# mLSTM heads: score order, the denominator's bank, table loads, and 1/sqrt by Ln and Exp

## The chip, the cores and the metric

One core of a Trainium2 chip runs the program; the other cores are idle. The metric is the device time of one execution in microseconds. The kernel before took 900.06 us, the median of three runs (899.17 to 901.06).

## What is computed

Two layers over 512 tokens of 1024 channels in fp32. The even layer makes one projection that feeds two groups of heads: A, four mLSTM heads of width 256, and B, eight stick-breaking attention heads of width 128. The odd layer is a pooling mixer. The change lies in group A:

```
q, k = silu(causal_dwconv(...)); ig, lf = gates
Sc  = (q k^T / 16) * W              # W = exp of gate sums, causal
num = Sc v ; den = sum over s of Sc
h   = num / max(|den|, exp(-m))
u   = sigmoid(oa) * h
ya  = u * rsqrt(mean(u*u) + eps) * hn_g * silu(za)
```

The kernel computes a head over all 512 tokens at once, without the chunks of the reference. With floor = exp(-m) and d = max(|den|, floor) it never divides by d: u is formed as num * sigmoid(oa), and the norm takes dd = mean(u*u) + eps*d*d, so that u / sqrt(dd) is the wanted quotient.

## The kernel before, in words

The token axis lies on the free dimension (512 columns, one PSUM bank), channels or keys on the 128 partitions. Every fp32 product is made of three fp32r matmuls over a high and a low half of each operand (mm3: L112 high x high, L113 high x low, L114 low x high). `split` makes the halves: ScalarE copies the high half (L88), VectorE subtracts it (L89).

PSUM's eight banks are shared out by tag: pj (2, projections), sc (2, scores), ac (2, accumulators), xa and xb (1 each). In the A stage xa serves `den` and the product "psb" of the two Strassen projections, xb serves "pse" and the mean `mn`; "psa" uses pj.

The loop at L722 runs over the four heads. For each: the projections of q and k (ps_qa), their causal convolution of four taps on VectorE (L428) and a Silu, then a Cast and a subtraction for the halves (L432, L433); the gate rows are loaded into `bc`; `values` projects v (psv_va, four blocks of 128 tokens, each split at L453); `mlstm`; `mlstm_den`; the output gate oa and the gate path za by `strassen2` (seven half-size products each, named psa, psb, pse); and `mlstm_out`. Values of head 0 are projected ahead of its q and k.

`mlstm` goes over four key blocks si. A block's scores s are six matmuls into a bank of tag sc, the tokens before the block left out (512, 384, 256 and 256 columns). ScalarE makes w = exp(bc + cT) (L476), VectorE multiplies it by the scores (L478), which is the last reader of the score bank, `split` makes ph and pl, and six matmuls add to the two num banks. GpSimd adds the w of all blocks (L492); that sum is split into dh and dl, and two matmuls by a matrix of ones make den (L495, L496). `mlstm_den` reads den with an Abs on ScalarE (L501).

`mlstm_out` takes the Sigmoid of o, forms u and its square mean (mn, L519 and L520), adds to dd (L521), takes the Sqrt on ScalarE and the reciprocal on VectorE (L523), the Silu of z, and stores the result in DRAM.

The order of work: a scheduler walks the program with a simulated clock, and each engine gets a fixed list from it; a tile with a tag waits until a buffer of that tag is free. `tc.add_manual_dep(later, earlier, NOSYNC)` adds an edge to that planning; on one engine it fixes the order of two instructions. Every activation that needs a table goes through `act`, which puts an ACT_TABLE_LOAD in front when the table set changes (L69) and links all of them in program order. Copy, Abs and Square go past `act` and need no load. In the kernel before, `last["ins"]` can name an instruction behind which the next table load must stand; it is set in one place only, at the end of the even layer (L800).

Of the kernel before, what the change touches and what calls it, by code (L numbers as in the profile page):

```python
# [9 lines left out]
AF = mybir.ActivationFunctionType  # L10
# [3 lines left out]
NOSYNC = mybir.DependencyInfo(mybir.DependencyClass.NoSync, mybir.DependencyReason.DATA)  # L14

P = 128
# [10 lines left out]
HA, HB = 4, 8  # L27
# [11 lines left out]
def body(nc, tc, x, pre_g, post_g, w_in, conv, b_i, b_f, hn_g, w_out, w_in_c, pool_w,  # L39
# [6 lines left out]
    with base as base, psum as psum, dram as dram:  # L46
# [5 lines left out]
        def sc(name): return bank("sc", 2, name)  # L52
        def ac(name): return bank("ac", 2, name)
        def xa(name): return bank("xa", 1, name)
# [1 line left out]

        table, last = {"ins": None, "set": None}, {}

        def link(i):
            if table["ins"] is not None:
# [3 lines left out]
        def act(dst, src, func, **kw):  # L66
            if table["set"] != TABLE[func]:
                table["set"] = TABLE[func]
                i = A.preload_act_table_set(TABLE[func])  # L69
                link(i)  # L70
                if "ins" in last:
                    tc.add_manual_dep(i.ins, last.pop("ins").ins.name, NOSYNC, reason="table order")
            i = A.activation(dst, src, func, **kw)
            link(i)
            return i
# [11 lines left out]
        def split(src, hi, lo, name=None):  # L87
            high[name] = A.activation(hi, src, AF.Copy)  # L88
            low[name] = V.tensor_tensor(lo, src, hi.bitcast(F32), op=ALU.subtract)  # L89
# [19 lines left out]

        def mm3(dst, lhs, rhs, first, last, **kw):  # L110
            (ah, al), (bh, bl) = lhs, rhs
            T.matmul(dst, lhsT=ah, rhs=bh, start=first, stop=False, **kw)  # L112
            T.matmul(dst, lhsT=ah, rhs=bl, start=False, stop=False, **kw)  # L113
            T.matmul(dst, lhsT=al, rhs=bh, start=False, stop=last, **kw)  # L114

        hTh = base.tile([P, 8, S], F32R, name="hTh")
        hTl = base.tile([P, 8, S], F32R, name="hTl")
# [192 lines left out]
        def phi(name): return at.tile([P, S], F32R, tag="phi", bufs=4, name=name)  # L310
        def plo(name): return at.tile([P, S], F32R, tag="plo", bufs=4, name=name)
# [124 lines left out]
        def values(col, name, with_gates=False):  # L436
            vh, vl = vtile(name)
            n = 264 if with_gates else 256

            def parts(t):  # L440
                yield nc.sync, t[:, :, :256], w_in[0, :, col:col + 256]
                if with_gates:
                    yield A, t[:, :, 256:], w_in[0, :, GI:GI + 8]
            w8 = load(parts, 8, n, name)
            w = [halves(w8[:, 4 * j:4 * j + 4], f"{name}{j}") for j in range(2)]
            for tt in range(NB):
                ps = pj(f"psv_{name}{tt}")
                for k in range(8):
                    wh, wl = w[k // 4]
                    ts = slice(tt * P, tt * P + P)  # L450
                    mm3(ps[:, :n], (hTh[:, k, ts], hTl[:, k, ts]),
                        (wh[:, k % 4], wl[:, k % 4]), k == 0, k == 7)
                split(ps[:, :256], vh[:, tt], vl[:, tt])  # L453
                if with_gates:
                    V.tensor_copy(gates[:, tt], ps[:, 256:n])
            return vh, vl
# [7 lines left out]

        def mlstm(h, q, k, v, bc):
            num = [ac(f"num{h}{j}") for j in range(2)]
            den = xa(f"den{h}")
            for si in range(NB):
                t0 = P * si
                n0 = min(t0, 256)  # L470
                s = sc(f"s{h}{si}")
                for j in range(2):
                    mm3(s[:, n0:], tuple(a[:, t0:t0 + P] for a in k[j]),
                        tuple(a[:, n0:] for a in q[j]), j == 0, j == 1)
                w = tmp(f"w{h}{si}")
                act(w[:, t0:], bc[:, ROW[si]:ROW[si] + S - t0], AF.Exp,  # L476
                    bias=cT[:, si, h:h + 1])
                V.scalar_tensor_tensor(w[:, t0:], s[:, t0:], 1.0 / 16.0, w[:, t0:],  # L478
                                       op0=ALU.mult, op1=ALU.mult)
                ph, pl = phi(f"ph{h}{si}"), plo(f"pl{h}{si}")  # L480
                if n0 < t0:
                    G.memset(ph[:, n0:t0].bitcast(F32), 0.0)
                    G.memset(pl[:, n0:t0].bitcast(F32), 0.0)
                split(w[:, t0:], ph[:, t0:], pl[:, t0:])
                first, last = si == 0, si == NB - 1
                for j in range(2):
                    mm3(num[j][:, n0:], tuple(a[:, si, j * P:j * P + P] for a in v),
                        (ph[:, n0:], pl[:, n0:]), first, last)
                if si == 0:
                    total = w  # L490
                else:
                    G.tensor_tensor(total[:, t0:], total[:, t0:], w[:, t0:], op=ALU.add)  # L492
            ph, pl = phi(f"dh{h}"), plo(f"dl{h}")
            split(total, ph, pl)
            T.matmul(den, lhsT=ones, rhs=ph, start=True, stop=False)  # L495
            T.matmul(den, lhsT=ones, rhs=pl, start=False, stop=True)  # L496
            return num, den
# [8 lines left out]
        def mlstm_out(h, num, dd, o, z):  # L506
            mn = xb(f"mn{h}")
            for j in range(2):
                act(o[j], o[j], AF.Sigmoid)
            us, squares = [], []  # L510
            for j in range(2):
                us.append(tmp(f"u{h}{j}"))
                squares.append(tmp(f"u2{h}{j}"))
                V.tensor_tensor(us[j], num[j], o[j], op=ALU.mult)
                A.activation(squares[j], us[j], AF.Square)
            V.tensor_tensor(squares[0], squares[0], squares[1], op=ALU.add)
            ph, pl = phi(f"uh{h}"), plo(f"ul{h}")
            split(squares[0], ph, pl)
            T.matmul(mn, lhsT=mean256, rhs=ph, start=True, stop=False)  # L519
            T.matmul(mn, lhsT=mean256, rhs=pl, start=False, stop=True)  # L520
            V.tensor_tensor(dd, mn, dd, op=ALU.add)  # L521
            act(dd, dd, AF.Sqrt)
            V.reciprocal(dd, dd)  # L523
            for j in range(2):
                c = 2 * h + j
                act(z[j], z[j], AF.Silu)
                V.scalar_tensor_tensor(us[j], us[j], hg(c), dd, op0=ALU.mult, op1=ALU.mult)
                V.tensor_tensor(z[j], us[j], z[j], op=ALU.mult)
                G.dma_start(ydr[:, c], z[j])
# [192 lines left out]
        for h in range(HA):  # L722
            if h == 0:
                v = values(VA, "va0")
            q, k = ([conv_silu(ps, co + 2 * h + j, f"{off}_{2 * h + j}") for j, ps in
                     enumerate(project2(w_in[0, :, off + 256 * h:off + 256 * h + 256],
                                        f"qa{off}_{h}"))] for off, co in ((QA, 0), (KA, 8)))
            bc = at.tile([P, EN + S], F32, tag="bc", bufs=1, name=f"bc{h}")
            nc.sync.dma_start(bc, rdr[h].partition_broadcast(P))
            for s in range(NB):  # L730
                t = bc[:, ROW[s]:ROW[s] + P]
                G.affine_select(t, t, pattern=[[1, P]], base=0, channel_multiplier=-1,
                                compare_op=ALU.is_ge, fill=-1e30)
            if h:
                v = values(VA + 256 * h, f"va{h}")
            num, den = mlstm(h, q, k, v, bc)
            dd = mlstm_den(h, den, bc)
            o, z = ([ozt(f"r_{n}{h}_{j}") for j in range(2)] for n in ("oa", "za"))
            if h == HA - 1:
                ready = y_split(y_back(tmp)(0, EVEN[0]), (qkt("yh_early"), qkt("yl_early")))  # L740
            for t, off, n in ((o, OA, "oa"), (z, ZA, "za")):
                strassen2(at, hs, w_in[0, :, off + 256 * h:off + 256 * h + 256], f"{n}{h}", t)
            mlstm_out(h, num, dd, o, z)
# [25 lines left out]
        with tc.tile_pool(name="odd", bufs=1) as od:  # L769
# [21 lines left out]
            def finish_even(ps, tt):  # L791
                xt = big(f"xe{tt}")
                nc.sync.dma_start(xt, xr[:, tt])
                t = big(f"xse{tt}")
                post(ps, t, gpo, xt, xn[:, tt], f"e{tt}")
                n0 = tt % 2 * P
                i = [copy() for copy in prenorm(xn[:, tt], t, tt, [gpr[:, :512], gpr[:, 512:]], f"p1{tt}", 1,
                            lambda i: y32[:, tt // 2 * 8 + 4 * i:tt // 2 * 8 + 4 * i + 4, n0:n0 + P])]
                if tt == NB - 1:
                    last["ins"] = i[-1]  # L800

            for a in range(2):
                finish_even(ps0[a], a)
# [112 lines left out]
```

## Time and profile before

| | |
|---|---|
| median of three runs | 900.06 us (899.17 to 901.06) |
| profiled execution | 899.45 us, span 897.5 us, granted TensorE clock 0.999 |
| TensorE matmul busy | 884.0 us (98%) |
| VectorE busy | 640.1 us (71%) |
| ScalarE busy | 521.1 us (58%), 28 table loads of 1.28 us |
| GpSimd busy | 99.0 us (11%) |

The span is from the first instruction to the last; the profiled execution's own time has 1.95 us around it. Matmuls are pipelined: a matmul's row shows when it starts and a modelled duration, and the next one starts before that is over. How far apart two starts are is therefore the time that a matmul takes in a full stream. The heads of group A take from about 250 to 500 us.

### The profile page before, as it was taken

To read this page: it belongs to the slowest core of one execution; us is meant where nothing else is said; L and a number is where in the kernel's file an instruction comes from. 1 tells how busy PE (TensorE), PEld (TensorE's weight loads), DVE (VectorE), ACT (ScalarE), POOL (GpSimd) and SP (SyncE) were. 2 spreads that over 40 slices of the span, in tenths; PEclk is the share of its full clock that TensorE was granted. 3 is DMA by queue.
4 is the path that set the end of the run, shared out by engine and by line. 5 is a ranking of instruction groups with operands and counts; after the bars stand their busy time and mean duration, and the time that the engine had idled before them with its cause. 6 is when DMAs were issued, how large, how long until landed. Compare 5 with 4: busy or idle time off the path is not lost.

```text
span 897.5 us, 13390 instructions
## 1 busy us (share of the span) xinstructions
PE 884.0 (98%) x5195; PEld 777.4 (87%) x5195; DVE 640.1 (71%) x969; ACT 521.1 (58%) x888; POOL 99.0 (11%) x209
## 2 busy tenths in 40 slices
PE   8999999999999999999999999999999999999997
PEld 6888889889988889999899888898999999988885
DVE  6655556567877697796796856779789897956542
ACT  7646676766766656746746835676455454655331
POOL 1001011101112101001001000005012120300000
PEclk9999999999999999999999999999999999999999
DMA  8231322222313431522422677641334242347331
GB/s 283 95 95 51 92 93 73 80 85 71 95 48 112 136 118 47 183 71 89 141 71 75 243 230 298 214 139 48 94 95 142 86 134 64 111 148 244 107 118 47
DMA packets 73202, 106.89 MB, mean 119 GB/s; under 512 B 3409, under 2 KB 59817, under 8 KB 73138
## 3 DMA queue, kind: packets, MB, share of 16 engines
q1 hardware_dynamic: 70240, 101.27, 34.1%
q0 software_dynamic: 1280, 4.20, 1.2%
q8 instruction: 41, 0.67, 0.3%
q10 hardware_dynamic: 1618, 0.56, 0.3%
q14 instruction: 23, 0.19, 0.1%
HBM read 99.70 MB, written 6.32 MB: 118 GB/s over the span
## 4 chain that ended last, share of the span: by engine, by line
PE 97%; DVE 1%; ACT 1%; issue 0%; POOL 0%; DVEq 0%; ACTq 0%; POOLq 0%
PE op L653 10%; PE oq L653 10%; PE ps_qa L112 3%; PE ps_qa L113 3%; PE ps_qa L114 3%; PE psv_va L112 2%; PE psv_va L114 2%; PE psv_va L113 2%; PE ps_zb L112 2%; PE mx L114 2%; PE mx L112 2%; PE mx L113 2%; PE ps_zb L114 2%; PE ps_kb L112 2%; PE ps_qb L114 2%; PE ps_kb L114 2%
## 5 line engine op out<-in xcount | busy, mean ns | idle before, releaser
L112 PE MATMUL ps_qa<-hTh,wh_qa 128*128 128x512 f32 x128 | 50.3, 393 | 0.0
L113 PE MATMUL ps_qa<-hTl,wh_qa 128*128 128x512 f32 x128 | 50.3, 393 | 0.0
L114 PE MATMUL ps_qa<-hTh,wl_qa 128*128 128x512 f32 x128 | 50.2, 393 | 0.0
L89 DVE TENSOR_TENSOR wl_wo_e<-w_wo_e,wh_wo_e 128x1024 fp32r<-128x1024 f32 x28 | 33.7, 1222 | 14.9 <-ACT wh_wo_e L88 14.7
L839 POOL TENSOR_TENSOR s<-s,invc 128x1 f32<-128x1 f32 (+3 forms) x16 | 22.2, 1385 | 188.6 <-DVE s L836 82.0
L88 ACT ACTIVATE wh_wo_e<-w_wo_e 128x1024 fp32r<-128x1024 f32 x28 | 28.9, 1055 | 22.4 <-DMA w_wo_e<-in_w_out_ab 14.3
L69 ACT ACT_TABLE_LOAD x28 | 35.9, 1283 | 1.8 <-PEq L901 1.4
L114 PE MATMUL psv_va<-wh_va,hTl 128*128 128x256 f32 x128 | 36.1, 282 | 0.0
L113 PE MATMUL psv_va<-wl_va,hTh 128*128 128x256 f32 x128 | 36.1, 282 | 0.0
L112 PE MATMUL psv_va<-wh_va,hTh 128*128 128x256 f32 x128 | 36.1, 282 | 0.0
L653 PE MATMUL op<-wl_wo_e,yh_e 128*128 128x512 f32 x112 | 36.1, 396 | 0.0
L653 PE MATMUL op<-wh_wo_e,yl_e 128*128 128x512 f32 x112 | 35.7, 395 | 0.0
L428 DVE SCALAR_TENSOR_TENSOR cv<-u,vecs,cv 128x511 f32<-128x511 f32 (+2 forms) x48 | 35.3, 738 | 0.1
L653 PE MATMUL op<-wh_wo_e,yh_e 128*128 128x512 f32 x112 | 34.8, 398 | 0.0
L89 DVE TENSOR_TENSOR wl_wo_o<-w_wo_o,wh_wo_o 128x1024 fp32r<-128x1024 f32 x20 | 24.2, 1223 | 11.0 <-ACT wh_wo_o L88 11.0
L653 PE MATMUL oq<-wh_wo_o,yl_o 128*128 128x512 f32 x96 | 30.6, 395 | 0.0
L653 PE MATMUL oq<-wl_wo_o,yh_o 128*128 128x512 f32 x96 | 30.5, 395 | 0.0
L653 PE MATMUL oq<-wh_wo_o,yh_o 128*128 128x512 f32 x96 | 29.6, 395 | 0.0
L88 ACT ACTIVATE wh_wo_o<-w_wo_o 128x1024 fp32r<-128x1024 f32 x20 | 20.8, 1053 | 15.2 <-PE oq L653 6.9
L112 PEld LDWEIGHTS ps_qa<-hTh,wh_qa 128*128 128x128 f32 x128 | 24.1, 188 | 5.4 <-ACT r_za L306 0.4
L114 PEld LDWEIGHTS ps_qa<-hTh,wl_qa 128*128 128x128 f32 x128 | 24.1, 188 | 5.2
L113 PEld LDWEIGHTS ps_qa<-hTl,wh_qa 128*128 128x128 f32 x128 | 24.1, 188 | 5.1
(559 smaller groups left out, 3238.0 us busy)
## 6 DMA issues: line engine op xcount, KB each, us to landing
w_wo_e<-in_w_out_ab SPq DMA_DIRECT2D x14, 1024.0 KB, 4.9
w_wo_o<-in_w_out_c SPq DMA_DIRECT2D x12, 1024.0 KB, 5.0
w_qa<-in_w_in_ab SPq DMA_DIRECT2D x8, 1024.0 KB, 4.9
w_p<-in_w_in_c SPq DMA_DIRECT2D x8, 1024.0 KB, 5.1
w_z<-in_w_in_c SPq DMA_DIRECT2D x8, 1024.0 KB, 5.0
w_qb<-in_w_in_ab SPq DMA_DIRECT2D x4, 1024.0 KB, 5.2
w_kb<-in_w_in_ab SPq DMA_DIRECT2D x4, 1024.0 KB
w_zb<-in_w_in_ab SPq DMA_DIRECT2D x4, 1024.0 KB
```

Source lines behind the costliest of these rows:

```text
L69: i = A.preload_act_table_set(TABLE[func])
L88: high[name] = A.activation(hi, src, AF.Copy)
L89: low[name] = V.tensor_tensor(lo, src, hi.bitcast(F32), op=ALU.subtract)
L112: T.matmul(dst, lhsT=ah, rhs=bh, start=first, stop=False, **kw)
L113: T.matmul(dst, lhsT=ah, rhs=bl, start=False, stop=False, **kw)
L114: T.matmul(dst, lhsT=al, rhs=bh, start=False, stop=last, **kw)
L428: V.scalar_tensor_tensor(acc[:, j:], u[:, :S - j], cw(3 - j, c), acc[:, j:], op0=ALU.mult, op1=ALU.add)
L653: T.matmul(ps[a][n], lhsT=l[:, ta], rhs=r[:, 0, n * 512:n * 512 + 512], start=(first and l is yh and r is wh), stop=(last and l is yl))
L839: G.tensor_tensor(sm[:, :e], sm[:, :e], invc[:, :e], op=ALU.mult)
```

## The change

- `mm3` returns its three matmuls. In `mlstm` an edge puts the first score matmul of block 1 behind the last one of block 0.
- `den` is taken from tag sc, after the four blocks, instead of from xa.
- `last` is renamed `hold` and set in two more places: in `mlstm` after every block's split (`high[None]` is the ScalarE copy of the last unnamed `split`), so that the head's next table load, that of the Sigmoid, stands behind the split of block 3; and, in heads 1 and 2, after `values`, so that the load for the head's Exps stands behind the split of the last block of values.
- `mlstm_out` makes 1/sqrt(dd) as exp(-ln(dd)/2) with two activations of one table set, instead of a Sqrt and a reciprocal.

```
         def mm3(dst, lhs, rhs, first, last, **kw):
             (ah, al), (bh, bl) = lhs, rhs
-            T.matmul(dst, lhsT=ah, rhs=bh, start=first, stop=False, **kw)
-            T.matmul(dst, lhsT=ah, rhs=bl, start=False, stop=False, **kw)
-            T.matmul(dst, lhsT=al, rhs=bh, start=False, stop=last, **kw)
+            return [T.matmul(dst, lhsT=ah, rhs=bh, start=first, stop=False, **kw),
+                    T.matmul(dst, lhsT=ah, rhs=bl, start=False, stop=False, **kw),
+                    T.matmul(dst, lhsT=al, rhs=bh, start=False, stop=last, **kw)]
...
         def mlstm(h, q, k, v, bc):
             num = [ac(f"num{h}{j}") for j in range(2)]
-            den = xa(f"den{h}")
             for si in range(NB):
...
-                for j in range(2):
-                    mm3(s[:, n0:], tuple(a[:, t0:t0 + P] for a in k[j]),
-                        tuple(a[:, n0:] for a in q[j]), j == 0, j == 1)
+                mms = [m for j in range(2)
+                       for m in mm3(s[:, n0:], tuple(a[:, t0:t0 + P] for a in k[j]),
+                                    tuple(a[:, n0:] for a in q[j]), j == 0, j == 1)]
+                if si == 1:
+                    tc.add_manual_dep(mms[0].ins, done.ins.name, NOSYNC, reason="order of scores")
+                done = mms[-1]
...
                 split(w[:, t0:], ph[:, t0:], pl[:, t0:])
+                hold["ins"] = high[None]
...
+            den = sc(f"den{h}")
             ph, pl = phi(f"dh{h}"), plo(f"dl{h}")
...
             V.tensor_tensor(dd, mn, dd, op=ALU.add)
-            act(dd, dd, AF.Sqrt)
-            V.reciprocal(dd, dd)
+            act(dd, dd, AF.Ln)
+            act(dd, dd, AF.Exp, scale=-0.5)
...
             if h:
                 v = values(VA + 256 * h, f"va{h}")
+                if h < HA - 1:
+                    hold["ins"] = high[None]
```

## Rows read from the trace of the kernel before

**Rows 1.** The page's busy times: busy us, share of the span, instructions.

```profile
PE 884.0 (98%) x5195; PEld 777.4 (87%) x5195; DVE 640.1 (71%) x969; ACT 521.1 (58%) x888; POOL 99.0 (11%) x209
```

**Rows 2.** TensorE's waits, 270 to 500 us: who for whom, us, times, longest.

```profile
PE s L112 <- DVE w L478: 2.6, 4, 0.7
PE psb_oa L112 <- ACT dd L501: 0.7, 1, 0.7
PE psb_za L112 <- DVE r_oa L291: 0.5, 1, 0.5
```

**Rows 3.** Timeline of TensorE, head 1: start us, duration, instruction [idle before, releaser].

```profile
342.66 0.40 PE L112 MATMUL s<-h,h 128*128 128x512 f32 x1
...
344.89 0.57 PE L114 MATMUL s<-h,l 128*128 128x512 f32 x2
345.30 0.39 PE L112 MATMUL s<-h,h 128*128 128x512 f32 x1
...
346.12 0.57 PE L114 MATMUL s<-h,l 128*128 128x512 f32 x2
347.38 0.39 PE L112 MATMUL s<-h,h 128*128 128x256 f32 x1 [0.68 <-DVE w L478]
347.60 0.28 PE L113 MATMUL s<-l,h 128*128 128x256 f32 x1
...
348.90 0.28 PE L112 MATMUL psa_oa<-n2h,wh_oa_b 128*128 128x256 f32 x1
...
350.32 0.63 PE L112 MATMUL num<-ph,vh_va 128*128 128x512 f32 x2
...
354.08 0.28 PE L114 MATMUL num<-ph,vl_va 128*128 128x256 f32 x1
```

**Rows 4.** Timeline of TensorE, head 0.

```profile
287.15 0.28 PE L114 MATMUL psa_za<-hTh,wl_za_a 128*128 128x256 f32 x1
287.99 0.39 PE L112 MATMUL s<-h,h 128*128 128x256 f32 x1 [0.57 <-DVE w L478]
...
296.47 0.40 PE L496 MATMUL den<-dl,ones 128*128 128x512 f32 x1
297.56 0.39 PE L112 MATMUL psb_oa<-hTh,wh_oa_a 128*128 128x256 f32 x1 [0.69 <-ACT dd L501]
...
298.97 0.28 PE L114 MATMUL psb_oa<-hTh,wl_oa_a 128*128 128x256 f32 x1
299.76 0.39 PE L112 MATMUL psb_za<-hTh,wh_za_a 128*128 128x256 f32 x1 [0.52 <-DVE r_oa L291]
```

**Rows 5.** Timeline of VectorE, head 1.

```profile
346.63 1.16 DVE L478 SCALAR_TENSOR_TENSOR w<-s,w 128x512 f32<-128x512 f32 x2 [1.82 <-PE s L114]
...
354.74 0.69 DVE L89 TENSOR_TENSOR dl<-w,dh 128x512 fp32r<-128x512 f32 x1 [1.02 <-ACT dh L88]
```

**Rows 6.** Timeline of ScalarE, head 1.

```profile
342.39 0.62 ACT L73 ACTIVATE cv<-cv 128x512 f32<-128x512 f32 x1
343.02 1.28 ACT L69 ACT_TABLE_LOAD   x1
344.32 1.93 ACT L73 ACTIVATE w<-bc,cT 128x512 f32<-128x512 f32 x4
346.26 1.28 ACT L69 ACT_TABLE_LOAD   x1
347.55 0.39 ACT L88 ACTIVATE vh_va<-psv_va 128x256 fp32r<-128x256 f32 x1
```

**Rows 7.** Groups of instructions by line: busy us, mean ns, idle before.

```profile
L523 DVE RECIPROCAL dd<-dd 128x512 f32<-128x512 f32 x4 | 13.4, 3346 | 0.0
```

**Rows 8.** Timeline of ScalarE, end of head 0 and start of head 1.

```profile
314.85 0.64 ACT L73 ACTIVATE dd<-dd 128x512 f32<-128x512 f32 x1
...
325.58 0.62 ACT L73 ACTIVATE cv<-cv 128x512 f32<-128x512 f32 x1
```

**Rows 9.** Busy times by stretch: length, PE, PEld, DVE, ACT, POOL (instructions), TensorE clock, DMA.

```profile
320.00:340.00 20.00, 20.00 (x129) 18.16 (x128) 20.00 (x33) 7.61 (x14) 1.46 (x4) 1.00 0.24 79
```

More of the change, by code (lines that the diff above doesn't have):

```diff
@@ L55, in xb @@
         def xb(name): return bank("xb", 1, name)
-        table, last = {"ins": None, "set": None}, {}
+        table, hold = {"ins": None, "set": None}, {}
         def link(i):
@@ L70, in act @@
                 link(i)
-                if "ins" in last:
-                    tc.add_manual_dep(i.ins, last.pop("ins").ins.name, NOSYNC, reason="table order")
+                if "ins" in hold:
+                    tc.add_manual_dep(i.ins, hold.pop("ins").ins.name, NOSYNC, reason="table order")
             i = A.activation(dst, src, func, **kw)
@@ L799, in finish_even @@
                 if tt == NB - 1:
-                    last["ins"] = i[-1]
+                    hold["ins"] = i[-1]
             for a in range(2):
```

## The prediction

> **What bounds the kernel now.** I read the page's busy shares first: TensorE is busy for 884.0 of the 897.5 us [rows 1]. Only what takes a wait or a matmul off TensorE's own list can shorten the run, and all the edits lie in the mLSTM stage. So the next view was TensorE's waits between 270 and 500 us. The reader is to see that there are six in all: four at the third score block of a head (score bank, waiting for VectorE's L478), one at psb_oa (waiting for ScalarE's Abs of the denominator) and one at psb_za (waiting for VectorE's L291) [rows 2]. They sum to 3.8 us between modelled ends and starts. The timeline says what they really take, because in a full stream matmuls start closer together than they last. A pair of 512 and 384 columns takes 0.41 us (344.89 to 345.30; two such pairs from there to 346.12), which by columns is 0.23 and 0.175; twelve of 256 columns take 1.42 (348.90 to 350.32), 0.12 each [rows 3].
>
> Head 1 [rows 3]: the pair of score matmuls at 346.12 is followed only at 347.38, 1.26 us later, so 0.85 is lost. The restarted matmul then takes 0.22 us to the next instead of 0.12, so 0.10 more. That is 0.95 us in head 1. Of the 2.6 us that the list gives to the four waits, 0.68 is head 1 and 0.57 head 0; the 1.35 left is 0.68 for each of heads 2 and 3, so I take 0.95 there too. In head 0 [rows 4] it is 287.99 - 287.15 - 0.12 = 0.72, and 0.10 for the restart: 0.82. After the denominator, 297.56 - 296.47 - 0.23 = 0.86 and 0.10: 0.96. Before psb_za, 299.76 - 298.97 - 0.12 = 0.67 and 0.10: 0.77. All six: 0.82 + 3 x 0.95 + 0.96 + 0.77 = 5.40 us. More than this the change can't give back.
>
> **Scores in order (edges from the last matmul of block 0 to the first of block 1).** No instruction is added. Today blocks 0 and 1 alternate, so that block 0 ends only one matmul ahead of block 1, and VectorE's L478 on block 0, which frees the bank for block 2, begins when TensorE has nothing left. In the new order all six matmuls of block 1 stand behind block 0's last. From the start of block 0's last matmul: VectorE begins 0.51 us later (346.12 to 346.63), needs 0.75 until TensorE can go on (346.63 to 347.38), 1.26 in all. TensorE meanwhile does that matmul and six of 384 columns: 0.23 + 6 x 0.175 = 1.28. The wait just vanishes, with nothing to spare, so I leave a restart of 0.10 in each head: gain 0.82 + 2.85 - 0.40 = 3.27 us. Block 3 comes behind block 2's six matmuls (0.7 us), while L478 on block 1, 384 columns wide, ends about 0.46 us after the first one (the pair takes 1.16 [rows 5]): no wait there.
>
> **Denominator in a score bank.** The two den matmuls write another bank; psb_oa no longer waits for ScalarE to read den: 0.96 us in head 0. Den needs the sum of all four w, so every L478, the last reader of the score banks, is over before it can start, and the next user of its bank is the next head's block 0: no wait is added. In heads 1 to 3 other products stand between den and psb_oa today and nothing waits [rows 2], so nothing is gained there. The 0.77 before psb_za stays in the sum: it is the one bank xa handed from one product to the next, and the edit does not touch that. It is the low end of the range.
>
> **Table loads.** Their number stays four a head. The Sigmoid load stands today between the Exps and the splits (346.26 [rows 6]); behind the last split it makes these 1.28 us earlier and itself later, and whatever follows in ScalarE's list has the same work ahead of it as before. No TensorE wait names those splits [rows 2], so there is nothing to gain; the other end is 4 x 1.28 = 5.1 us lost, if TensorE came to wait for what stands behind the load in each head. I take 0, by the unchanged amount of work. In heads 1 and 2 the Exp load moves behind the last values split. That split runs after the Silu ending at 343.01: split to 343.41, load to 344.69, first Exp of 512 columns (0.64) to 345.35, against 344.32 + 0.64 = 344.96 now. Queued behind it on ScalarE are the four Exps; VectorE's L478 waits for them. With the scores where they are now, block 0's last matmul starts at 344.89 + 3 x 0.23 = 345.58 and L478 can begin at 346.09, so 0.7 us of cover is left: cost 0. If that cover is gone the price is in the first rival below.
>
> The row shows no more than the load itself: Silu ends 343.01, load starts 343.02, first Exp 344.32, 0.02 us after the load's end [rows 6]. The Trainium skill (ScalarE: Activation LUTs, What ACT_TABLE_LOAD costs) gives a switch 1283 ns for the load and about 1380 ns of drain, 2.66 us; the load agrees with the trace, the drain is not there. By that rule the first Exp would end at 346.73, L478 start at 346.78 and block 2 at 347.53 instead of 346.86: 0.67 and 0.10 lost in each of two heads, and the time 897.3.
>
> **Ln and Exp for Sqrt and reciprocal.** VectorE loses 4 x 3.35 = 13.4 us [rows 7]; ScalarE gets four more 512-column activations of 0.64 (the Sqrt's row [rows 8]), 2.6 us. The chain from dd to its use becomes 0.64 + 3.35 - 2 x 0.64 = 2.7 us shorter a head, but no TensorE wait names what follows. The Silu load and the two Silus come 0.64 us later. Today they end at about 314.85 + 0.64 + 1.28 + 2 x 0.62 = 318.0, and the next Silu in the fixed order starts at 325.58 [rows 8], so 7.5 us hide it. VectorE has no idle time in the 20 us after the reciprocal [rows 9] and TensorE waits for none of its work there, so a lighter VectorE gives it nothing at once. It may bring the last key's halves forward by up to 2.7 us, and what that can cost is rival A. Late next, once the waits are gone, is L478 on block 0 again, which has nothing to spare.
>
> **Sum.** 3.27 + 0.96 = 4.23 us. The profiled execution took 899.45 (span 897.5 and 1.95 around it): 895.2. It was 0.6 under the median of the runs, 900.06, so as a median: 895.8. All six waits gone would be 894.7.
>
> **Rivals.**
> A. The held Exp load takes the place of the bank wait. Lighter VectorE makes the keys ready up to 2.7 us sooner, so heads 1 and 2 can issue blocks 0 and 1 without the 12 product matmuls (1.42 us) that now stand between 342.66 and 344.89. Then block 0 ends near 344.2 and block 1's slots end at 342.66 + 6 x 0.23 + 6 x 0.175 = 345.09, but L478 waits for the Exp until 345.40 and block 2 for L478 until 346.15: 1.06 + 0.10 = 1.16 lost instead of 0.95. Against the forecast 2 x (1.16 - 0.10) = 2.1 us: 897.9. For it: the cover is 0.7 us and VectorE is full just before. Against it: with xa free, psb_oa (12 matmuls) is one more product that can stand there. 0.18; the table drain, with the row against it, 0.02.
> B. No change: the list is planned anew from a simulated clock, and new waits of about 1 us turn up in as many places as were removed. For it: today's four are such misses of a plan. Against it: elsewhere in 225 us this planner left only the waits listed. About 900.0; 0.15.
> C. Slower: fill is spent early. Between the last score and the first num stand 12 product matmuls (348.90 to 350.32), and between the last num (354.08) and the end of the denominator's low half (354.74 + 0.69 = 355.43) others fill 1.2 us [rows 3, 5]. The free xa bank lets products go ahead sooner; if these two gaps are left bare in heads 1 to 3, each head loses 1.4 + 1.2 + 0.2 of restarts = 2.8, together 8.4: 895.8 + 8.4 = 904.2. It decides from 1.4 us a head, half of that. Against it: the two Strassen projections are fourteen products a head, and psb_oa comes behind den today [rows 4]. 0.09.
>
> **How the numbers follow.** Forecast 0.56, A and the drain 0.20, B 0.15, C 0.09. About 0.2%, 1.8 us, is what a measurement here can tell from no change; faster by more (under 898.3) is the forecast and A: 0.76. Same 0.15, slower 0.09. The range goes from all six waits gone with a run 0.8 below the median, 893.9, up past A to within B, 899.9; about 0.17 lies above it.
>
> **What would show it.** TensorE's list of waits for the stage: L112 on L478 gone or at most 0.1 a head, psb_oa on ScalarE gone; psb_za may remain. All of block 0 ahead of block 1 in each head. 28 table loads as now, the Sigmoid load behind the four ph splits. No reciprocal of 512 columns, VectorE some 13 us less busy, ScalarE 2.6 more. Rival A shows as L112 waiting for L478, and L478 for an Exp; C as num or den waiting for a split. The prediction is wrong if TensorE's waits in the stage sum to more than 2 us, or if the saving comes from outside it.

## The result, and the profile after

The changed kernel takes 895.0 us (median of four runs, 894.49 to 895.55) against 899.8 us for the kernel before on the same chip: a ratio of 0.9937, 95% interval 0.9925 to 0.9949. The forecast was 895.8. The profiled execution has a span of 892.4 us, 5.1 less than before.

The page's busy times (busy us, share of the span, instructions): TensorE does the same work and VectorE 13.3 us less. ScalarE's busy time is unchanged, where 2.6 us more were forecast: its activations of dd do take 2.5 us more (9.9 against 7.4), but busy time counts rows that overlap only once, and what took up the difference was not traced.

```profile
PE 883.2 (99%) x5195; PEld 777.8 (87%) x5195; DVE 626.8 (70%) x965; ACT 521.1 (58%) x892; POOL 99.6 (11%) x209
```

TensorE's waits of the changed kernel from 270 us to the end (who for whom, us in total, times, longest). All six of [rows 2] are gone, and what is left lies in the odd layer, where it was before:

```profile
PE ps_p L112 <- ACT hTh L88: 0.2, 1, 0.2
PE ps_p L113 <- DVE hTl L89: 0.2, 1, 0.2
PE ps_p L112 <- ACT p L830: 0.2, 1, 0.2
```

Head 1 in TensorE's timeline, against [rows 3]. Block 0 (341.06 on), block 1 (342.45 on), then 12 matmuls of the product psa_oa, then block 2 (344.94), with no idle time:

```profile
341.06 0.40 PE L112 MATMUL s<-h,h 128*128 128x512 f32 x1
...
342.21 0.39 PE L114 MATMUL s<-h,l 128*128 128x512 f32 x1
342.45 0.34 PE L112 MATMUL s<-h,h 128*128 128x384 f32 x1
...
343.51 0.28 PE L112 MATMUL psa_oa<-hTh,wh_oa_a 128*128 128x256 f32 x1
...
344.94 0.28 PE L112 MATMUL s<-h,h 128*128 128x256 f32 x1
```

ScalarE (against [rows 6]) and VectorE (against [rows 5]) in that head. The last values split (341.26) now stands ahead of the Exp load, the Sigmoid load (348.07) behind the four ph splits, and the last key's low half is done at 337.96, 3.1 us before the first score:

```profile
341.26 0.38 ACT L88 ACTIVATE vh_va<-psv_va 128x256 fp32r<-128x256 f32 x1 [0.36 <-PE psv_va L114]
341.66 1.28 ACT L69 ACT_TABLE_LOAD   x1
342.95 1.92 ACT L73 ACTIVATE w<-bc,cT 128x512 f32<-128x512 f32 x4
...
347.45 0.61 ACT L88 ACTIVATE ph<-w 128x256 fp32r<-128x256 f32 x2
348.07 1.28 ACT L69 ACT_TABLE_LOAD   x1
```

```profile
337.27 0.69 DVE L433 TENSOR_TENSOR l<-cv,h 128x512 fp32r<-128x512 f32 x1
...
343.71 1.16 DVE L480 SCALAR_TENSOR_TENSOR w<-s,w 128x512 f32<-128x512 f32 x2 [1.22 <-PE s L114]
```

L480 is the old L478. The row names the score matmul as its releaser, but block 0's last matmul ended at 342.21 + 0.39 = 342.60, while the first Exp (0.64 of the 1.92) ended at 342.95 + 0.64 = 343.59: by these times it was the Exp that VectorE waited for.

**A measure for the comparisons.** Span differences of a few tenths can't be read across kernels, because the opening varies: the first matmul of the first ps_qb starts between 37.06 and 38.36 us in the fourteen profiles, although TensorE's list up to there is the same in all of them. The part behind it, up to the first ps_qa matmul, is 212.86 to 212.92 us. So I use the stretch from the first ps_qa matmul to the first transposition at the end of the even layer (tp_p from xse): the four heads and the first half of the output projection. It goes from 249.93 to 558.90 before, 308.97 us, and in the changed kernel:

```profile
249.99 0.39 PE L112 MATMUL ps_qa<-hTh,wh_qa 128*128 128x512 f32 x1
...
553.89 1.04 PE L205 MATMUL tp_p<-ident,xse 128*128 128x128 f32 x8
```

303.90 us, 5.07 less; what follows, up to the last matmul, differs by at most about 0.5 us between any two profiles. Each kernel has one profile, so each stretch is of one execution.

### The profile page after: what moved, and what is told of

Read it like the earlier page. It is cut to its first block, busy times and chain, and to the rows that moved or that the text cites. A ratio compares the mean times of both kernels' runs of the same rounds, so it can differ in the third digit from the quotient of the medians.

```text
span 892.4 us, 13383 instructions
## 1 busy us (share of the span) xinstructions
PE 883.2 (99%) x5195; PEld 777.8 (87%) x5195; DVE 626.8 (70%) x965; ACT 521.1 (58%) x892; POOL 99.6 (11%) x209
## 4 chain that ended last, share of the span: by engine, by line
PE 94%; DMA 3%; ACT 1%; DVE 1%; issue 0%; SPq 0%; DVEq 0%; ACTq 0%
PE oq L657 10%; PE op L657 8%; PE ps_qa L114 3%; PE ps_qa L113 3%; PE ps_qa L112 3%; PE psv_va L112 2%; PE psv_va L114 2%; PE psv_va L113 2%; PE ps_zb L112 2%; PE mx L114 2%; PE mx L113 2%; PE mx L112 2%; PE ps_zb L114 2%; PE ps_kb L112 2%; PE ps_qb L114 2%; PE ps_qb L112 2%
```

## The experiments

Twelve kernels, each timed in three rounds; the kernel before had medians of 900.1 to 900.7 us beside them. "Stretch" is the measure above, against 308.97 before and 303.90 after.

| kernel | edits | median us | ratio to before (95%) | stretch us |
|---|---|---|---|---|
| only_order | score edge | 898.94 | 0.9989 (0.9979 to 0.9998) | 308.50 |
| only_bank | den in a score bank | 902.39 | 1.0024 (1.0013 to 1.0035) | 312.71 |
| only_hold | both table loads | 901.09 | 1.0010 (1.0000 to 1.0019) | 309.68 |
| only_lnexp | Ln and Exp | 898.07 | 0.9974 (0.9965 to 0.9984) | 307.05 |
| no_order | all but the edge | 895.35 | 0.9939 (0.9922 to 0.9955) | 304.70 |
| no_bank | all but the bank | 899.61 | 0.9991 (0.9981 to 1.0000) | 308.62 |
| no_hold | all but the table loads | 895.26 | 0.9939 (0.9924 to 0.9954) | 304.73 |
| no_lnexp | all but Ln and Exp | 896.27 | 0.9951 (0.9937 to 0.9966) | 305.92 |
| order_sig | edge, Sigmoid load | 899.77 | 1.0001 (0.9987 to 1.0015) | 309.83 |
| bank_lnexp | bank, Ln and Exp | 898.01 | 0.9965 (0.9952 to 0.9978) | 306.88 |
| order_bank | edge, bank | 897.78 | 0.9968 (0.9956 to 0.9979) | 307.05 |
| fill_late | all, products held back | 896.24 | 0.9954 (0.9938 to 0.9970) | 305.68 |

**The edge alone (only_order).** Kernel before, with

```
+                if si == 1:
+                    tc.add_manual_dep(mms[0].ins, done.ins.name, NOSYNC, reason="order of scores")
+                done = mms[-1]
```

> The kernel before with the score edge alone; den stays in bank xa, Sqrt and reciprocal and table loads as before. Its TensorE list: in heads 1 to 3 blocks 0, 1, 2, 3 stand one behind the other (12 product matmuls inside block 0), in head 0 likewise. Theory 'one edit, one wait' (the forecast): block 1's six matmuls cover L478 (1.28 against 1.26 us), so the four waits for L478 (2.6 us in the list, 3.67 with restarts) fall to 0.1 each at most, psb_oa and psb_za stay at 0.7 and 0.5; span 897.5 - 3.3 = 894.2. Rival 'fill' (the waits go only where the planner has other matmuls to put between blocks 1 and 2, which this list lacks): waits stay over 0.4 each, span above 896.

The four waits for L478 are gone, but the stretch is only 0.47 us shorter. TensorE's waits of that kernel from 270 us (first four rows):

```profile
PE psa_oa L112 <- ACT pt_oa L289: 1.2, 3, 0.4
PE psb_oa L112 <- ACT dd L504: 0.7, 1, 0.7
PE psb_za L112 <- DVE r_oa L291: 0.5, 1, 0.5
PE psa_za L112 <- ACT wh_za_a L88: 0.3, 1, 0.3
```

Its TensorE, VectorE and ScalarE in head 1:

```profile
345.01 0.39 PE L114 MATMUL s<-h,l 128*128 128x512 f32 x1
...
346.30 0.35 PE L112 MATMUL s<-h,h 128*128 128x256 f32 x1
...
347.19 0.38 PE L112 MATMUL s<-h,h 128*128 128x256 f32 x1
...
347.88 0.28 PE L114 MATMUL s<-h,l 128*128 128x256 f32 x1
```

```profile
345.51 0.69 DVE L481 SCALAR_TENSOR_TENSOR w<-s,w 128x512 f32<-128x512 f32 x1 [0.94 <-PE s L114]
346.58 0.56 DVE L481 SCALAR_TENSOR_TENSOR w<-s,w 128x384 f32<-128x384 f32 x1 [0.37 <-PE s L114]
```

```profile
346.03 1.28 ACT L69 ACT_TABLE_LOAD   x1
...
348.12 0.38 ACT L289 ACTIVATE pt_oa<-psa_oa 128x256 f32<-128x256 f32 x1
```

The predicted cover is there to the hundredth: L478 (here L481) begins 0.50 us after block 0's last matmul, and block 2 starts 1.29 after it (forecast 0.51 and 1.28). But the next product adds to a bank that ScalarE's copy pt_oa has to read first, and this copy stands behind the Sigmoid load and ends at 348.50, so TensorE loses 0.55 and 0.10 for a restart in each of heads 1 to 3, and 0.5 in head 0 for wh_za_a. In the kernel before, the copy was nearly as late:

```profile
348.36 0.38 ACT L289 ACTIVATE pt_oa<-psa_oa 128x256 f32<-128x256 f32 x1
```

It ended at 348.74 there, only 0.16 us before its product at 348.90 [rows 3]. The wait was moved by one step, not removed.

Block 3, for which the prediction saw no wait, is late too: with the blocks in order, L481 on block 1 can't follow the one on block 0 at once, but begins at 346.58, after block 1's own last matmul, and block 3 starts at 347.19. In each of heads 1 to 3 this is 0.12 of waiting and 0.10 of restart, too small for the list of waits; here the later wait for pt_oa covers it.

**The Sigmoid load added (order_sig).** Only_order, with

```
                 split(w[:, t0:], ph[:, t0:], pl[:, t0:])
+                hold["ins"] = high[None]
```

> The kernel before with the score edge and the Sigmoid load held behind the last split, and nothing else. With the edge alone the four waits for L478 went, and psa_oa came to wait for ScalarE's copy pt_oa (1.2 us in the list, 3 times, 0.65 each with the restart), which stood behind the Sigmoid load. 'Load in the way': with the load behind the splits the copy comes 1.28 us earlier and those three waits go; den stays in xa, so psb_oa (0.7) and psb_za (0.5) still wait; span 896.6 - 3 x 0.65 = 894.7. Rival 'copy late anyway' (it waits for the VectorE and the splits ahead of it, not for the load): the three waits stay, span 896.6 within 0.3.

"Load in the way" is right on its wait: no matmul waits for pt_oa any more. It is wrong on the time: the stretch is 1.33 us longer than with the edge alone, because the new list has other waits, in head 0 (num for pl, den for dl), in heads 2 and 3 (psa_za for the copy pt_za, 0.3 in the list) and at the projection (op for yh_e):

```profile
PE op L657 <- ACT yh_e L88: 0.6, 1, 0.6
...
PE num L113 <- DVE pl L89: 0.3, 1, 0.3
PE den L500 <- DVE dl L89: 0.2, 1, 0.2
```

**The bank alone (only_bank).** Kernel before, with

```
-            den = xa(f"den{h}")
...
+            den = sc(f"den{h}")
```

> The kernel before with den in a score bank alone. Its list has blocks 0 and 1 alternating as before and block 2 behind them at once in heads 2 and 3 (two product matmuls between in head 1); psb products stand ahead of the scores. 'One edit, one wait': psb_oa's wait for den goes (1.0 us), the four for L478 stay; span 896.5, or 895.7 if psb_za's goes too because the products moved. 'Fill': the free psb products stand where the waits were and take those too; span 892.5 to 894.

Slower, which no theory had. The waits at psb_oa and psb_za are gone and those for L478 stay, as "one edit, one wait" says, but new losses cost more: 1.9 us where the projection starts, then about 2 us in the next 6, and in the heads 0.75 at pse_oa and 0.55 at ps_qa. Its waits (first four), and ScalarE, VectorE and TensorE at the projection:

```profile
PE s L112 <- DVE w L477: 2.4, 4, 0.7
PE op L653 <- ACT wh_wo_e L88: 1.7, 1, 1.7
PE pse_oa L114 <- DVE wl_oa_b L89: 0.6, 1, 0.6
PE ps_qa L112 <- ACT r_za L306: 0.4, 1, 0.4
```

```profile
506.34 1.33 ACT L88 ACTIVATE yh_e<-yt 128x512 fp32r<-128x512 f32 x2 [1.46 <-DMA yt<-ydr]
...
508.21 1.28 ACT L69 ACT_TABLE_LOAD   x1
...
510.56 1.04 ACT L88 ACTIVATE wh_wo_e<-w_wo_e 128x1024 fp32r<-128x1024 f32 x1
```

```profile
508.31 3.35 DVE L523 RECIPROCAL dd<-dd 128x512 f32<-128x512 f32 x1
511.63 1.23 DVE L89 TENSOR_TENSOR wl_wo_e<-w_wo_e,wh_wo_e 128x1024 fp32r<-128x1024 f32 x1
```

```profile
511.65 1.19 PE L653 MATMUL op<-wh_wo_e,yh_e 128*128 128x512 f32 x4 [1.70 <-ACT wh_wo_e L88]
512.91 0.73 PE L653 MATMUL op<-wl_wo_e,yh_e 128*128 128x512 f32 x2
513.48 1.01 PE L653 MATMUL op<-wh_wo_e,yl_e 128*128 128x512 f32 x2
514.28 1.05 PE L653 MATMUL op<-wl_wo_e,yh_e 128*128 128x512 f32 x2
```

The first op matmul waited until 511.65 for the high half of its weights. ScalarE reached that copy only at 510.56, behind a wait for a transfer (yt, to 506.34), the Sqrt, a table load and two Silus; the reciprocal is not in that list. The next wait, at 512.91, is for the low half (0.34). VectorE makes it right behind the 3.35 us reciprocal (to 511.66), but could not have made it earlier, because the high half it needs was ready only at 511.60: at this place the reciprocal costs next to nothing.

What follows is no wait at all. Pairs of 512 columns start 0.80 to 0.86 us apart instead of 0.46, and the view by stretch (as in [rows 9]) shows a granted clock of 0.51, the lower of TensorE's two levels (1.2 GHz instead of 2.4):

```profile
513.48:516.85 3.37, 3.37 (x10) 2.61 (x9) 3.37 (x6) 2.91 (x4) 0.52 (x1) 0.51 0.18 13
```

Before the clock fell, TensorE had stood for 1.9 us ahead of 511.65. This costs about 1.6 us of the 3.74. No other of the fourteen profiles has such a fall between its first and its last 20 us. It is not in every execution of this kernel: of its seven timed runs five have a mean granted clock of 0.996, and the two with 0.998 took 901.25 and 901.50 us, still above the 900.14 of the kernel before.

**The bank with Ln and Exp (bank_lnexp).** Only_bank, with

```
-            act(dd, dd, AF.Sqrt)
-            V.reciprocal(dd, dd)
+            act(dd, dd, AF.Ln)
+            act(dd, dd, AF.Exp, scale=-0.5)
```

> The kernel before with den in a score bank and Ln and Exp; no score edge, no table-load edit. Its TensorE list at the start of the output projection is the same as with the bank alone, where op waited 1.9 us at 509 us for weights whose low half stood behind the 3.35 us reciprocal on VectorE, with five more stalls of about 0.4 behind it. 'Reciprocal in the way': those go, 1.9 + 5 x 0.3 = 3.4 us; blocks 1 and 2 have 12 or more product matmuls between them in heads 1 and 2, none in heads 0 and 3, so L478 is waited for once or twice (1.0 each); span 902.1 - 3.4 - 2 = 896.7 or less. Rival 'early projection' (op starts before its weights' transfers and high halves are there, whatever VectorE does): the 1.7 in the list stays, span over 899.

The stretch falls by 5.83 us against the bank alone, to 306.88. At the projection 3.9 us become 1.2. "Reciprocal in the way" does not explain this: the wait for the low half is 0.34 here as it was there, without a reciprocal, and about 1.6 of the 3.9 was the lower clock, which this profile does not have. The wait for ScalarE's high half is still there (0.6 in the list instead of 1.7), so "early projection" is right in kind; why it is shorter is not shown, since ScalarE's list is another one too. In the heads the waits at pse_oa are gone. One wait for L478 is left, in head 0, where block 2 stands right behind blocks 0 and 1; in heads 1 and 2 product matmuls stand between, and in head 3 the blocks follow one another without a wait. The largest sum in the list is now that of ps_qa for ScalarE's r_za (1.0 in two waits).

**Ln and Exp alone (only_lnexp).** The same two lines, in the kernel before.

> The kernel before with Ln and Exp for Sqrt and reciprocal alone. VectorE busy 13 us less, ScalarE 2.5 more. 'One edit, one wait': nothing on TensorE, 897.5, six waits. 'Fill': the keys come earlier and the list of head 1 has 12 product matmuls between blocks 1 and 2, so that head's wait goes (0.95 us): 896.5.

The stretch is 1.92 us shorter. Head 1's wait is gone, where 12 product matmuls now stand between blocks 1 and 2; those of heads 2 and 3 are 0.5 instead of 0.85. "Fill" is right, "nothing" is wrong.

**The table loads alone (only_hold).** Both `hold` lines, in the kernel before.

> The kernel before with the two table-load edits alone. 'One edit, one wait': nothing, 897.5, all six waits there. 'Fill': the list now has 22 product matmuls between blocks 1 and 2 in head 0 and none there in heads 1 to 3, so head 0's wait for L478 goes (0.8 us) and three stay: 896.7.

0.71 us longer. Head 0's wait for L478 is gone as "fill" said, but that head now waits for the denominator's halves instead (0.4 and 0.2 in the list), and heads 1 to 3 still wait for L478 (2.1, three times).

**Each edit left out of the whole.**

> The changed kernel without the score edge. Its list still has block 0 ahead of block 1 in heads 1 to 3 and 12 product matmuls before block 2; only in head 0 do the blocks alternate, with 32 product matmuls before block 2. 'One edit, one wait': without the edge the four waits for L478 return, span 892.4 + 3.3 = 895.7. 'Fill': no wait in any head, span 892.4 within 0.3; the edge adds nothing once the other edits are there.

> The changed kernel with den back in bank xa. Its list has psb_oa right behind den in head 0 and psb_za right behind psb_oa, as in the kernel before. Both theories: psb_oa waits for ScalarE again (0.7 in the list, 0.96 us) and psb_za for L291 (0.5, 0.77). 'One edit, one wait': nothing else, span 892.4 + 1.7 = 894.1. 'Fill' (the psb products fill the L478 gaps): waits for L478 return too where fewer products stand between, up to 3.7 more, 897.8.

> The changed kernel without the two table-load edits in the heads. Its list has block 2 directly behind block 1 in heads 0 and 2, and 4 to 5 product matmuls between in heads 1 and 3. 'One edit, one wait': nothing, span 892.4. 'Fill': with block 2 directly behind block 1 L478 decides; waits of 0 to 0.5 in heads 0 and 2, span 892.4 to 893.6.

> The changed kernel with Sqrt and reciprocal instead of Ln and Exp. Its list has blocks 0 to 3 one behind the other in heads 1 to 3 with 12 product matmuls inside block 0. 'One edit, one wait': nothing for TensorE, waits at most 0.1 a head, span 892.4 to 892.8. 'Early keys' (the lighter VectorE is what lets blocks 0 and 1 and the fill stand in order): waits for L478 of 0.3 to 0.9 a head return in heads 1 to 3, span 893.5 to 895.

Without the edge no matmul waits for L478 in any head: the planner puts block 0 ahead of block 1 by itself in heads 1 to 3. The stretch is 0.80 us longer, about half of it at op, which waits for the high half of its weights at 507.39 (0.53 with the restart), and half in head 1, where psa_za waits for wh_za_a (0.45). Without the table loads it is 0.83 longer: op waits in the same way (0.46), and the rest is small stalls, among them 0.20 at block 3 of head 0 and 0.30 at a ps_qa. Neither is told from the changed kernel by its timed runs. Without the bank 4.72 us of the 5.07 are lost. Its waits in head 0 (TensorE's timeline, only rows with a wait):

```profile
296.84 0.36 PE L113 MATMUL num<-pl,vh_va 128*128 128x256 f32 x1 [0.31 <-DVE pl L89]
...
298.16 0.50 PE L500 MATMUL den<-dl,ones 128*128 128x512 f32 x1 [0.23 <-DVE dl L89]
...
299.35 0.38 PE L112 MATMUL psb_oa<-hTh,wh_oa_a 128*128 128x256 f32 x1 [0.69 <-ACT dd L505]
...
301.55 0.38 PE L112 MATMUL psb_za<-hTh,wh_za_a 128*128 128x256 f32 x1 [0.52 <-DVE r_oa L291]
```

With what is lost behind them these are 0.55, 0.49, 1.06 and 0.78 us; 0.61 at psa_za in head 0 and 0.86 at op make it 4.35 of the 4.72. L478 is not in the list of waits, but the timeline shows it once: in head 2 block 2 comes 0.35 us late at 411.05, because VectorE waited for the Exp. So of the 4.72 the bank's own two waits are 1.84. Without Ln and Exp the stretch is 2.02 us longer; two waits carry 1.4 of it:

```profile
PE psa_za L112 <- ACT ph L88: 0.6, 1, 0.6
PE pse_oa L114 <- DVE wl_oa_b L89: 0.3, 1, 0.3
```

The rest are stalls too small for the list: at the same pse_oa in heads 1 and 2 (0.29 and 0.28) and at block 3 there (0.22 each). "Early keys" has the time right (span 894.2) but not the place, for block 2 waits nowhere. The wait at pse_oa shows what the reciprocal does. In head 3 the high half wh_oa_b is ready at 453.48, and its low half begins 2.6 us later:

```profile
456.09 1.23 DVE L89 TENSOR_TENSOR wl_oa_b<-ws_oa,wh_oa_b 128x1024 fp32r<-128x1024 f32 x1
```

VectorE has no idle time from the start of the reciprocal (443.37) to there, so the reciprocal delays all that stands behind it; in the changed kernel the same row begins 0.8 us behind its high half, and nothing waits.

**The edge and the bank (order_bank).**

> The kernel before with the score edge and den in a score bank; Sqrt, reciprocal and table loads as before. 'One edit, one wait': 897.5 - 3.7 - 1.7 = 892.1 to 893, as the changed kernel. 'Next wait': L478 and psb waits gone, but ScalarE's copy pt_oa still stands behind the Sigmoid load and the reciprocal ahead of the projection's weights, so 1 to 4 us of those come in: span 894 to 898.

A stretch of 307.05. "Next wait" is right in kind, though not in which: in heads 2 and 3 the wait for L478 has moved to block 3 (0.77 and 0.79, waiting for block 1's bank, because VectorE puts a weight's low half, 1.22 us, between its L480 on blocks 0 and 1), and in head 1 psa_za waits for vl_va (0.74).

**Products held back (fill_late).** The changed kernel, with an edge in heads 1 and 2 from block 2's last score matmul to the first product of oa and of za:

```
+                if si == 2:
+                    scored[h] = done
...
+                    if name in ("oa1", "oa2", "za1", "za2") and k == 0 and start:
+                        then(scored[int(name[2])], ms[0])
```

> The changed kernel with one more edge in heads 1 and 2: the first products of oa and za stand behind block 2's scores, so that blocks 0, 1 and 2 follow one another directly. In the changed kernel 12 product matmuls (1.43 us) stand between blocks 1 and 2 there. Rival A of the prediction (the held Exp load decides once that cover is gone): L478 still begins about 0.2 us after block 1's last slot, so block 2 waits 0.95 and 0.10 for the restart in each of the two heads: L112 on L478 with 1.4 to 1.8 us in the list, 2 times, span 892.4 + 2.1 = 894.5. Forecast's account (the six matmuls of block 1 are cover enough): waits of 0.1 at most, span 892.4 to 892.8.

TensorE, VectorE and ScalarE in head 1:

```profile
340.60 0.34 PE L114 MATMUL s<-h,l 128*128 128x384 f32 x1
341.72 0.39 PE L112 MATMUL s<-h,h 128*128 128x256 f32 x1 [0.78 <-DVE w L486]
341.94 0.28 PE L113 MATMUL s<-l,h 128*128 128x256 f32 x1
```

```profile
340.97 1.16 DVE L486 SCALAR_TENSOR_TENSOR w<-s,w 128x512 f32<-128x512 f32 x2 [1.22 <-PE s L114]
```

```profile
340.21 1.92 ACT L73 ACTIVATE w<-bc,cT 128x512 f32<-128x512 f32 x4
```

341.72 - 340.60 - 0.17 = 0.95 and 0.10 for the restart, in heads 1 and 2 each; the stretch is 1.78 us longer. Rival A's price is right (1.05 measured, 1.16 forecast), and by the times it is the Exp that decides: its first ends at 340.85, L478 (here L486) begins at 340.97, a full microsecond after block 0's last matmul, which ran from 339.48 to 339.87. In the changed kernel the 12 product matmuls hide just this.

## Why the prediction was right, and where its sum was not

**The total.** Six waits of 5.40 us stood on TensorE's path, all six went, and 5.07 us came back. Reading the stage's waits first, and pricing each from start to start with its restart, was the step that carried the forecast (4.23 us, and 5.40 as the end that the range had to hold). About the difference to 5.40 is lost again in small stalls, the largest at the projection: op starts 0.34 us late at 507.03, waiting for the low half of its weights.

That the sum came out near is partly luck. It gave all of the gain to the edge and the bank, and nothing to the other two edits. Edge and bank together (order_bank) give back 1.92 us; the two edits set at nothing bring the other 3.15.

**Scores in order, 3.27 us: the mechanism right, the term wrong.** The edge alone does what was worked out for block 2, and the stretch gains 0.47 us by it, because a copy behind the Sigmoid load was ready only 0.16 us before the product that needs it, hidden by the wait for L478. The sentence that named L478 on block 0 as the next one late is the step that failed: a wait list shows the last release only, and I did not look for the next product's own inputs. The sentence on block 3 ("no wait there") was wrong too: it took L478 on block 1 to follow the one on block 0, as in the old order, and in the new one block 1 ends later (0.22 us a head in only_order). In the whole, the edge is worth 0.80 us by one profile, and none of that at L478: in heads 1 to 3 the cover is 12 product matmuls, not block 1; only in head 0 does block 2 stand right behind block 1.

**Denominator's bank, 0.96 us: mis-sized.** Alone it costs 3.74 us, about 1.6 of them by the lower clock in that execution; in the whole it is worth 4.72. Psb_oa's and psb_za's waits went as soon as xa was free, psb_za's too, which I had left in the sum. The rest is in other places of the list. My reading is that the free bank lets the planner put every psb product elsewhere, and so changes all lists up to the projection; no run tests this.

**Table loads, 0.** Not zero: the Sigmoid load in front of pt_oa costs 0.65 us in each of three heads once the scores are in order. But held back alone, or with the edge, it shifts waits rather than removing them (0.71 and 0.86 us longer than before); in the whole it is worth 0.83 at most. The rule of the Trainium skill (ScalarE: Activation LUTs, What ACT_TABLE_LOAD costs) that a switch also costs 1380 ns of drain does not show after the change either: the load at 341.66 ends at 342.94, the Exp starts at 342.95.

**Ln and Exp, 0.** Worth 1.92 us alone and 2.02 in the whole. That no TensorE wait named the reciprocal was true of the list as it stood, and no longer once the order changed: at the start of a head VectorE's 3.35 us stand ahead of weight halves that the new TensorE list wants sooner (1.1 us at pse_oa in three heads, without Ln and Exp). Alone, its gain lies in the waits for L478, in lists that were planned anew.

**Rivals.** A's premise came true: in head 1 above, blocks 0 and 1 stand directly one behind the other, L478 waits for the Exp, and the keys are ready 3.1 us before the first score (0.15 without Ln and Exp). Its price was shown with the products held back. A product in the gap is why it cost nothing, though not the psb_oa that was named against it: it is psa_oa, which stood among the matmuls of blocks 0 and 1 before. B shows wherever an edit stands alone: the lists are planned anew, and waits of the same size appear elsewhere. C's mechanism, fill gone where num and den want it, was not seen in the whole; without the bank head 0 has it, at num and den, 1.04 us.

**What stays open.** The edits don't add up: alone they give 0.47, -3.74, -0.71 and 1.92, together 5.07. Why the planner's lists come out as they do was not traced; each list was only read. That the edge and the table loads are worth anything in the whole rests on one profile each, and the losses of order_sig and the table loads alone (0.86 and 0.71) hardly show in their timed runs.

## What to carry to other kernels

When a list of work is planned as a whole, add up the waits on the bound engine to see what a change can give back, but do not assign them to edits: ask of each what else the instruction behind the wait needs, and when that would be ready. A bank shared by one late reader and several products can cost more than the waits that show at it (here 1.84 of 4.72 us). A long instruction on an engine that nobody waits for (a 3.35 us reciprocal) may still be worth removing: here it was the best single edit. And before a row of late matmuls is called a row of waits, read the granted clock of that stretch.
